# Token sums and Strassen weights at one common byte place in their tiles

## The chip, the cores and the metric

The kernel runs on one core of a Trainium2 chip. A core has a matrix engine (TensorE, PE in the profile, whose weight loads are listed apart as PEld), a vector engine (VectorE, DVE), a scalar engine (ScalarE, ACT), GpSimd (POOL) and a synchronisation engine (SP) from which most transfers are issued. Its on-chip memory has 128 partitions, and every tile is a run of bytes at the same address of each partition; matrix products land in a second memory, PSUM. The metric is the device time of one launch in microseconds (us), lower is better.

## The reference

A two-layer encoder on 512 tokens of width 1024, in 32-bit floats. Each layer has a feed-forward block, a mixer (attention of several kinds in layer 0, banded attention in layer 1), attention to a memory of 256 tokens, and a second feed-forward block. The change touches the four feed-forward blocks:

```python
def rmsnorm(x, g):
    y = x * rsqrt(mean(x * x, axis=-1) + EPS)
    return y * g

def swiglu(x, wg, wu, wd):          # x 512 x 1024, wg and wu 1024 x 2816, wd 2816 x 1024
    return (silu(x @ wg) * (x @ wu)) @ wd

for layer in range(2):
    h = h + 0.5 * swiglu(rmsnorm(h, g1), wg1, wu1, wd1)
    h = h + mixer(rmsnorm(h, gm))
    h = h + memory_attention(rmsnorm(h, gx), rmsnorm(mem, gs))
    h = h + 0.5 * swiglu(rmsnorm(h, g2), wg2, wu2, wd2)
```

## The kernel before

**Products.** Activations are held transposed (features on partitions, tokens along the row). Every 32-bit number that goes into a matrix product is split into a leading part and a rest, and a product of two such numbers is three passes: leading by leading, leading weights by rest of the tokens, and rest of the weights by leading tokens. Tiles whose name ends in `h` hold leading parts, those that end in `l` hold rests: `wh`/`wl` and `sh`/`sl` are weights (two buffers of the first pair, one of the second, used in turn), `xh`/`xl` are tokens. For a weight tile, ScalarE writes the leading part and VectorE the rest, from a raw tile `wf`, `s1` or `s3` that a transfer has filled. In the profile `ps_pa<-xh,wh` is a matmul that streams 256 or 512 columns of `xh` past 128 x 128 weights of `wh` into the PSUM tile `ps_pa`; each matmul has its own weight load.

**A feed-forward block.** The 22 blocks of 128 hidden features are taken in 11 pairs. The first pair (`plain_pair`, L325) is computed directly. The other ten are computed by Strassen's scheme (`open_pair`, `sum_pair`, `cross_pair`, `close_pair`): tokens, input features and gate/up weights are each cut in two, and seven products of half size take the place of eight. Each of the seven is a call of `product` (L452), 24 matmuls of 256 columns: two output blocks, three passes, four blocks of 128 input features. Three of the seven use token parts as they are (`xh`, `xl`, called "11", "21" and "22"), four use sums or differences of token parts (`t1h`, `t1l` to `t4h`, `t4l`). The sums are made once per block in `token_sums`. The weights of a product are the raw quarters (`wf`) or sums of two quarters, which a transfer that adds into the tile, ScalarE and VectorE make (`s1`, `s3`). After some pairs come matmuls of the down projection (`down_products`, L585, 512 columns), in three chunks.

**Order.** The order of TensorE's instructions is the order in which the code issues them; that of the others is set by a scheduler that works from due times. On TensorE a pair is followed by the next in this order: 11, t1, t2, 21, t3, then 11 of the next pair, t4, 22, t1, t2 and so on. So token parts and token sums alternate, but for t1 and t2, which follow each other. In each block ten pairs give 70 products, 280 in the whole program.

**Places.** In what follows the place of an operand is its first byte's address in a partition modulo 512, counted in units of 64 bytes, from 0 to 7. Tiles of 512, 1024 or 2048 numbers take a multiple of 512 bytes, and so do the weight tiles, which are 128 numbers longer than needed (`WIDE`, 1152 numbers, 4608 bytes). So what stands at a tile's start has place 0, and every block of 128 weights or 256 tokens in it has the same place as its first. `operand` (L422) puts a product's weights `place` times 64 bytes (`LINE`, 16 numbers) into their tiles, and `X_PLACE` and `SUM_PLACE` say where:

- products with token parts: tokens at place 0, leading weights at 1, rests at 3;
- products with token sums: tokens at place 1, leading weights at 2, rests at 4. The sums lie in a pool of their own (`f.sp`), whose first tile, `line`, is 64 bytes long and holds nothing;
- all other large matmuls (L325, L585, L638, L687): both operands at place 0.

Of the kernel before, what the change touches and what calls it, by code (L numbers as in the profile page):

```python
# [11 lines left out]
F32 = mybir.dt.float32  # L12
F32R = mybir.dt.float32r
# [6 lines left out]
P = 128  # L20
# [44 lines left out]

LINE = 16
WIDE = 1024 + 8 * LINE
X_PLACE = (1, 3)
SUM_PLACE = (2, 4)

LEAD, REST = ((0, 0), (0, 1)), ((1, 0),)

# [39 lines left out]
class Encoder:  # L112
# [158 lines left out]
    def ffn(self, pre):  # L271


        with ExitStack() as ctx:
            pool = lambda name: ctx.enter_context(self.tc.tile_pool(name=pre + name, bufs=1))
            f = self.f = SimpleNamespace(pre=pre, ctx=ctx, hp=pool("h"), tp=pool("t"), sp=pool("s"), H={}, n=0, last=None)
            R = self.plain_pair()
            ends = [sum(CHUNKS[:c + 1]) // 2 for c in range(len(CHUNKS))]
            c = 0
            pair = self.open_pair(1)  # L280
            R()
            for p in range(1, FB // 2):
                final = p == FB // 2 - 1
                self.sum_pair(pair)
                if p in ends:
                    self.down(c)
                    c += 1
                self.cross_pair(pair)
                if final:
                    early = self.block(c, 0, True)  # L290
                    self.down_products(c, early, LEAD + REST, False)
                    self.close_pair(pair, True)
                    self.down(c, early)
                else:
                    old, pair = pair, self.open_pair(p + 1)
                    self.close_pair(old, False)
                if self.mem_r is None:
                    self.mem_stats(p)
# [71 lines left out]
    def token_sums(self):  # L370


        nc, f = self.nc, self.f
        xs, gain = self.xs, self.col(self.norm)
        half = KB // 2
        one, two = slice(0, 256), slice(256, 512)
        part = lambda t, k: t[:, (k % half) * 256:(k % half) * 256 + 256]
        g = lambda k: gain[:, k:k + 1]

        def combine(out, k, tokens, op, other):  # L380
            nc.vector.scalar_tensor_tensor(part(out, k), self.x[k][:, tokens], g(k), part(other, k), op0=OP.mult, op1=op)

        def parts(name, t, sign=1.0):
            after = None if name == "t1" else f.lowered if name == "t2" else f.gated
            with self.behind(f.factored), self.behind(after):
                h = f.sp.tile([P, 1024], F32R, name=name + "h", tag=name + "h")
                nc.scalar.activation(h, t, AF.Copy, scale=sign)
                l = f.sp.tile([P, 1024], F32R, name=name + "l", tag=name + "l")
                if sign == 1.0:
                    nc.vector.tensor_sub(l, t, h.bitcast(F32))  # L390
                else:
                    nc.vector.scalar_tensor_tensor(l, t, sign, h.bitcast(F32), op0=OP.mult, op1=OP.subtract)
            return [(part(h, k), part(l, k)) for k in range(half)]

        f.sp.tile([P, LINE], F32, name="line", tag="line")
        lead, rest = range(half), range(half, KB)
        room = [f.tp.tile([P, 2048], F32, name="tq", tag="gu", bufs=2) for _ in range(2)]
        t1, t2, x12, t3 = (t[:, o:o + 1024] for t in room for o in (0, 1024))
        for k in lead:
            nc.scalar.activation(part(x12, k), self.x[k][:, two], AF.Copy, scale=g(k))  # L400
        for k in lead:
            combine(t1, k, one, OP.subtract, x12)
        for k in rest:
            combine(t2, k, two, OP.add, t1)
        for k in rest:
            combine(t3, k, two, OP.subtract, x12)
        t4 = x12
        for k in rest:
            combine(t4, k, one, OP.subtract, t2)
        quarters = lambda ks, tokens: [tuple(x[:, tokens] for x in xs[k]) for k in ks]  # L410
        f.B = {"11": quarters(lead, one), "21": quarters(rest, one), "22": quarters(rest, two),
               "1": lambda: parts("t1", t1, -1.0), "2": lambda: parts("t2", t2),
               "3": lambda: parts("t3", t3), "4": lambda: parts("t4", t4)}

    def tokens(self, name):
# [3 lines left out]
            B[name] = B[name]()  # L419
        return B[name]  # L420

    def operand(self, t, place, own=None):  # L422

        nc, f = self.nc, self.f
        if own is None:
            own = f.n % 3 == 2
            f.n += 1
        h, l = [(f.tp if own else self.wp).tile([P, WIDE], F32R, name=n, tag=n, bufs=1 if own else 2)[:, o * LINE:o * LINE + 1024]
                for n, o in zip(("sh", "sl") if own else ("wh", "wl"), place)]
        self.leading = nc.scalar.activation(h, t, AF.Copy)  # L430
        self.parted = nc.vector.tensor_sub(l, t, h.bitcast(F32))  # L431
        return h, l
# [30 lines left out]
    def open_pair(self, p):  # L463
        nc, f = self.nc, self.f
        pair = SimpleNamespace(p=p)
        pair.y = self.bank("pa")
        with self.tc.high_priority():
            pair.w11 = self.raw_quarter(p, 0)
            w = self.operand(pair.w11, X_PLACE)
        self.product(pair.y, w, self.tokens("11"), True)  # L470
        pair.gu = f.tp.tile([P, 2048], F32, name="gu", tag="gu", bufs=2)
        nc.scalar.copy(self.corner(pair, 0, 0), self.halves(pair.y))
        return pair

    def sum_pair(self, pair):

        nc, f, p = self.nc, self.f, pair.p
        pair.z = self.bank("pb")
        with self.tc.high_priority():
            pair.s = f.tp.tile([P, 1024], F32, name="s1", tag="s1", bufs=2)  # L480
            self.fetch(pair.s, p, 3)
            nc.gpsimd.dma_start(pair.s, self.quarter(p, 2), accum_op=OP.add)  # L482
            w = self.operand(pair.s, SUM_PLACE)
        with self.tc.high_priority():
            xs = self.tokens("1")
        self.product(pair.z, w, xs, True)
        with self.tc.high_priority():
            f.lowered = nc.vector.tensor_sub(pair.s, pair.s, pair.w11)
            xs = self.tokens("2")
            w = self.operand(pair.s, SUM_PLACE)  # L490
            f.lowered = self.parted
        self.product(pair.y, w, xs, False)
        nc.scalar.copy(self.corner(pair, 0, 1), self.halves(pair.y))

    def cross_pair(self, pair):
        nc, f, p = self.nc, self.f, pair.p
        with self.tc.high_priority(), self.behind(f.lowered if p == 1 else None):
            pair.w12 = self.raw_quarter(p, 1)
            w = self.operand(pair.w12, X_PLACE)
        x = self.bank("pa")  # L500
        self.product(x, w, self.tokens("21"), True)
        c = self.corner(pair, 0, 0)
        nc.vector.tensor_add(c, c, self.halves(x))
        with self.tc.high_priority():
            s = f.tp.tile([P, 1024], F32, name="s3", tag="s3", bufs=2)
            self.fetch(s, p, 2)
            with self.behind(f.led):
                nc.scalar.activation(s, s, AF.Copy, scale=-1.0)  # L508
            nc.gpsimd.dma_start(s, self.quarter(p, 0), accum_op=OP.add)  # L509
            w = self.operand(s, SUM_PLACE)  # L510
        self.product(pair.y, w, self.tokens("3"), False)
        c = self.corner(pair, 1, 1)
        nc.scalar.copy(c, self.halves(pair.y))
        nc.vector.tensor_add(c, c, self.halves(pair.z))

    def close_pair(self, pair, final):
        nc, f, p = self.nc, self.f, pair.p
        own = False if final else None

        def lower():  # L520
            with self.tc.high_priority():
                w = self.operand(self.raw_quarter(p, 3), SUM_PLACE, own)
            self.product(pair.y, w, self.tokens("4"), False)
            nc.scalar.copy(self.corner(pair, 1, 0), self.halves(pair.y))

        def upper():
            with self.tc.high_priority():
                nc.vector.tensor_sub(pair.s, pair.w12, pair.s)
                w = self.operand(pair.s, X_PLACE, own)
            self.product(pair.z, w, self.tokens("22"), False)  # L530
            c = self.corner(pair, 0, 1)
            nc.vector.tensor_add(c, c, self.halves(pair.z))
# [1027 lines left out]
```

## Time and profile before

| what | value |
|---|---|
| median of three runs | 2098.28 us (2096.92 to 2098.28) |
| the profiled execution | 2099.43 us, span of its instructions 2097.7 us |
| mean granted TensorE clock | 0.996 |
| TensorE busy | 2064.1 us, 98% of the span |
| weight loads busy | 1843.6 us, 88% |
| VectorE busy | 1522.2 us, 73% |
| ScalarE busy | 1141.7 us, 54% |
| transfers | 279.64 MB, 133 GB/s over the span |

A busy matrix engine is not one at its peak: matmuls overlap, so the duration of one (276 ns and more for 256 columns) is longer than the time from its start to the start of the next. The pace is read from the starts, in the timeline. There a row is a run of matmuls of one kind: start in us, time from the first one's start to the last one's end, engine, line, tiles and shapes, and the count.

### The profile page before, as it was taken

What the parts mean: (1) busy time and instruction counts of PE and PEld (TensorE: products, weight loads), DVE (VectorE), ACT (ScalarE), POOL (GpSimd) and SP (SyncE); (2) the same over time, 40 slices, a digit from 0 to 9 for tenths busy, and PEclk for the clock granted to TensorE, in tenths of its full rate; (3) what the DMA queues carried; (4) which work ended last, traced back from release to release, by engine and by line L of the source; (5) the groups of instructions that cost most, each with busy time, mean ns of one, the idle gap of its engine ahead of it and who ended that gap; (6) DMA issues with size and microseconds to landing.
All of it is one profiled execution on the core that took longest, in us unless ns stands there. A gap on an engine that the chain in (4) does not pass through costs nothing.

```text
span 2097.7 us, 32478 instructions
## 1 busy us (share of the span) xinstructions
PE 2064.1 (98%) x12834; PEld 1843.6 (88%) x12834; DVE 1522.2 (73%) x2198; ACT 1141.7 (54%) x1706; POOL 363.2 (17%) x319
## 2 busy tenths in 40 slices
PE   8999999999999999999999999999999999999999
PEld 7989898877788889898989899988888888989997
DVE  8758577589876697685789576675668688857666
ACT  7636345466686575362556354354778566626443
POOL 1101003345431120000020000013453022000000
PEclk9999999999999999999999999999999999999999
DMA  7746535222241266474356466344224225646633
GB/s 236 209 125 179 149 101 181 90 68 69 81 133 62 73 181 181 128 194 131 99 170 175 131 171 181 98 125 149 91 80 131 91 71 151 171 130 180 171 101 93
DMA packets 86120, 279.64 MB, mean 133 GB/s; under 512 B 9680, under 2 KB 12880, under 8 KB 85968
## 3 DMA queue, kind: packets, MB, share of 16 engines
q1 hardware_dynamic: 74448, 235.62, 34.4%
q0 software_dynamic: 11520, 41.95, 11.3%
q8 instruction: 101, 1.65, 0.3%
q14 instruction: 51, 0.42, 0.1%
HBM read 271.24 MB, written 6.29 MB: 132 GB/s over the span
## 4 chain that ended last, share of the span: by engine, by line
PE 89%; DVE 7%; ACT 1%; issue 1%; DMA 1%; POOL 0%; SPq 0%; DVEq 0%; ACTq 0%; POOLq 0%
PE ps_pa L452 26%; PE ps_pa L687 11%; PE ps_pb L452 11%; PE ps_pa L585 11%; PE ps_pb L585 10%; PE ps_pa L638 4%; PE ps_pa L325 3%; PE ps_pb L793 2%; PE ps_pa L1234 2%; PE ps_pb L845 1%; PE ps_pa L1084 1%; PE ps_pb L818 1%; PE ps_pb L638 1%; PE ps_pa L1003 1%; PE ps_pb L325 1%
## 5 line engine op out<-in xcount | busy, mean ns | idle before, releaser
L163 ACT ACTIVATE wh<-wf 128x1024 fp32r<-128x1024 f32 (+2 forms) x211 | 215.2, 1021 | 349.6 <-PE ps_pa L585 97.0
L165 DVE TENSOR_TENSOR wl<-wf,wh 128x1024 fp32r<-128x1024 f32 (+2 forms) x169 | 200.2, 1187 | 49.0 <-ACT wh L163 47.5
L431 DVE TENSOR_TENSOR wl<-s,wh 128x1024 fp32r<-128x1024 f32 x108 | 132.0, 1222 | 67.1 <-ACT wh L430 67.1
L430 ACT ACTIVATE wh<-s 128x1024 fp32r<-128x1024 f32 x108 | 114.4, 1059 | 101.0 <-PE ps_pb L452 35.1
L430 ACT ACTIVATE wh<-wf 128x1024 fp32r<-128x1024 f32 x84 | 88.9, 1059 | 94.7 <-PE ps_pa L452 32.3
L509 POOL DMA_DIRECT2D s<-l_ffn_wq x40 | 35.6, 889 | 528.8 <-ACT s L508 460.8
L165 POOL TENSOR_TENSOR wl<-wf,wh 128x1024 fp32r<-128x1024 f32 x42 | 101.9, 2426 | 141.5 <-ACT wh L163 139.9
L687 PE MATMUL ps_pa<-wh,xh 128*128 128x512 f32 x384 | 123.6, 403 | 0.0
L687 PE MATMUL ps_pa<-wh,xl 128*128 128x512 f32 x384 | 119.9, 393 | 0.0
L687 PE MATMUL ps_pa<-wl,xh 128*128 128x512 f32 x384 | 119.5, 393 | 0.0
L482 POOL DMA_DIRECT2D s<-l_ffn_wq x40 | 35.7, 892 | 437.6 <-PE ps_pa L452 148.1
L431 DVE TENSOR_TENSOR wl<-wf,wh 128x1024 fp32r<-128x1024 f32 x84 | 102.5, 1220 | 6.3 <-ACT wh L430 3.4
L595 DVE TENSOR_TENSOR dn<-ps_pa,R 128x512 f32<-128x512 f32 x48 | 33.1, 689 | 93.2 <-PE ps_pa L585 92.9
L585 PE MATMUL ps_pb<-hh,wh 128*128 128x512 f32 x352 | 95.5, 389 | 0.0
L585 PE MATMUL ps_pb<-hl,wh 128*128 128x512 f32 x352 | 95.4, 389 | 0.0
L585 PE MATMUL ps_pb<-hh,wl 128*128 128x512 f32 x352 | 95.4, 389 | 0.0
L230 POOL TENSOR_TENSOR acc<-acc,sq 128x512 f32<-128x512 f32 (+1 forms) x37 | 51.2, 1383 | 251.5 <-ACT sq L229 250.4
L431 DVE TENSOR_TENSOR sl<-s,sh 128x1024 fp32r<-128x1024 f32 x52 | 64.0, 1232 | 39.5 <-ACT sh L430 39.4
L585 PE MATMUL ps_pa<-hh,wh 128*128 128x512 f32 x328 | 88.8, 390 | 0.0
L585 PE MATMUL ps_pa<-hh,wl 128*128 128x512 f32 x328 | 88.6, 389 | 0.0
L585 PE MATMUL ps_pa<-hl,wh 128*128 128x512 f32 x328 | 88.6, 389 | 0.0
L687 PEld LDWEIGHTS ps_pa<-wh,xl 128*128 128x128 f32 x384 | 72.8, 190 | 16.2
(376 smaller groups left out, 5846.8 us busy)
## 6 DMA issues: line engine op xcount, KB each, us to landing
wf<-l_ffn_wq SPq DMA_DIRECT2D x120, 512.0 KB, 4.0
s<-l_ffn_wq SPq DMA_DIRECT2D x80, 512.0 KB, 4.9
s<-l_ffn_wq POOLq DMA_DIRECT2D x80, 512.0 KB, 7.0
wf<-l_ffn_wd SPq DMA_DIRECT2D x64, 512.0 KB, 4.2
wf<-l_w_in SPq DMA_DIRECT2D x48, 512.0 KB, 3.3
wf<-l_ffn_wd SPq DMA_DIRECT2D x32, 384.0 KB, 3.1
wf<-l_mem_wkv SPq DMA_DIRECT2D x16, 512.0 KB, 3.3
wf<-l_w_out SPq DMA_DIRECT2D x16, 512.0 KB, 3.3
```

The source lines that it names most:

```text
L163: self.leading = nc.scalar.activation(wh[:, sl], w[:, sl], AF.Copy)
L165: eng.tensor_sub(wl[:, sl], w[:, sl], wh.bitcast(F32)[:, sl])
L230: self.summed = (eng or nc.gpsimd).tensor_add(acc[:, :n], acc[:, :n], sq[:, :n])
L325: nc.tensor.matmul(p, w[a][:, k * P:(k + 1) * P], xs[k][c], start=k == order[0] and a == c == 0, stop=k == order[-1] and a == 1)
L430: self.leading = nc.scalar.activation(h, t, AF.Copy)
L431: self.parted = nc.vector.tensor_sub(l, t, h.bitcast(F32))
L452: self.nc.tensor.matmul(bank[:, sl], w[a][:, o:o + P], xs[k][b], start=first and z == a == b == k == 0, stop=z == a == 1 and k == KB // 2 - 1,
L585: self.nc.tensor.matmul(bank, w[a][:, j * P:(j + 1) * P], h, start=j == a == e == 0, stop=j == nb - 1 and (a, e) == ops[-1])
L638: nc.tensor.matmul(banks[dd], a[:, o:o + P], parts(k)[b], start=k == first and a is wh and b == 0, stop=k == last and a is wl)
L687: nc.tensor.matmul(banks[i], xs[k][a][:, i * P:(i + 1) * P], w[b][:, kk * 512:kk * 512 + 512], start=k == a == b == 0, stop=k == KB - 1 an ...
L793: nc.tensor.matmul(bank[:, o:o + n], a, b[:, :n], start=c == 0, stop=c == len(ops) - 1)
L1234: nc.tensor.matmul(p, ws[z][a][:, k * P:(k + 1) * P], xs[k][b], start=k == order[0] and a == b == 0, stop=k == order[-1] and a == 1)
```

## The change

One place for all Strassen products: the token sums now lie in the pool of the block's other tiles (`f.tp`), where each tile starts at a multiple of 512 bytes, and `operand` puts all weights at places 1 and 3. So the products with token sums have tokens at place 0 and weights at 1 and 3, as those with token parts had and have. Within a product the distance from tokens to weights is what it was, 64 and 192 bytes.

```diff
-X_PLACE = (1, 3)
-SUM_PLACE = (2, 4)
+PLACE = (1, 3)
...
-            f = self.f = SimpleNamespace(pre=pre, ctx=ctx, hp=pool("h"), tp=pool("t"), sp=pool("s"), H={}, n=0, last=None)
+            f = self.f = SimpleNamespace(pre=pre, ctx=ctx, hp=pool("h"), tp=pool("t"), H={}, n=0, last=None)
...
         def parts(name, t, sign=1.0):
...
-                h = f.sp.tile([P, 1024], F32R, name=name + "h", tag=name + "h")
+                h = f.tp.tile([P, 1024], F32R, name=name + "h", tag=name + "h")
                 nc.scalar.activation(h, t, AF.Copy, scale=sign)
-                l = f.sp.tile([P, 1024], F32R, name=name + "l", tag=name + "l")
+                l = f.tp.tile([P, 1024], F32R, name=name + "l", tag=name + "l")
...
-        f.sp.tile([P, LINE], F32, name="line", tag="line")
...
-    def operand(self, t, place, own=None):
+    def operand(self, t, own=None):
...
-                for n, o in zip(("sh", "sl") if own else ("wh", "wl"), place)]
+                for n, o in zip(("sh", "sl") if own else ("wh", "wl"), PLACE)]
...
-            w = self.operand(pair.s, SUM_PLACE)
+            w = self.operand(pair.s)
...
-            w = self.operand(pair.w12, X_PLACE)
+            w = self.operand(pair.w12)
```

In the same way every other call of `operand` loses its `place`. With the pool gone, some tiles of a block get other addresses: `t1h` moves from byte 192576 to 175104, `sh` from 175104 to 191488, `s3` from 184320 to 200704, `t3h` from 208960 to 208896. `wh`, `wl`, `wf`, `s1`, `xh` and `xl` stay.

No instruction is added, removed or put elsewhere in its queue, on any engine. What each waits for is the same too, but at one place: in the first feed-forward block of layer 1, TensorE waits once for the transfers that filled the tiles of the block before (the names that begin with `DMA`). Before, it did so ahead of t2's first product:

```order
L343 MATMUL ps_pb<-ident,factor 128x128 x3
L452 MATMUL ps_pb<-t1h,wh 128x256 [waits Activation_49]
L452 MATMUL ps_pb<-t1h,wh 128x256 x3
L452 MATMUL ps_pb<-t1l,wh 128x256 [waits DVE_49]
...
L452 MATMUL ps_pb<-t1h,wl 128x256 x4
L452 MATMUL ps_pa<-t2h,sh 128x256 [waits DMAHW0_49,DMASW7_49,DMAHW1_49,DMASW6_49,DMAHW2_49,DMASW5_49,DMAHW3_49,DMASW4_49,DMAHW4_49,DMASW3_49,DMAHW5_49,DMASW2_49,DMAHW6_49,DMASW1_49,DMAHW7_49,DMASW0_49,Activation_49]
L452 MATMUL ps_pa<-t2h,sh 128x256 x3
```

Now it does so ahead of t1's (lines are two lower in the changed file):

```order
L342 MATMUL ps_pb<-ident,factor 128x128 x3
L450 MATMUL ps_pb<-t1h,wh 128x256 [waits DMAHW0_49,DMASW7_49,DMAHW1_49,DMASW6_49,DMAHW2_49,DMASW5_49,DMAHW3_49,DMASW4_49,DMAHW4_49,DMASW3_49,DMAHW5_49,DMASW2_49,DMAHW6_49,DMASW1_49,DMAHW7_49,DMASW0_49,Activation_49]
L450 MATMUL ps_pb<-t1h,wh 128x256 x3
L450 MATMUL ps_pb<-t1l,wh 128x256 [waits DVE_49]
...
L450 MATMUL ps_pb<-t1h,wl 128x256 x4
L450 MATMUL ps_pa<-t2h,sh 128x256 [waits Activation_49]
L450 MATMUL ps_pa<-t2h,sh 128x256 x3
```

The same 16 waits, for the same transfers, stand 24 matmuls earlier.

More of the change, by code (lines that the diff above doesn't have):

```diff
@@ L468, in open_pair @@
             pair.w11 = self.raw_quarter(p, 0)
-            w = self.operand(pair.w11, X_PLACE)
+            w = self.operand(pair.w11)
         self.product(pair.y, w, self.tokens("11"), True)
@@ L489, in sum_pair @@
             xs = self.tokens("2")
-            w = self.operand(pair.s, SUM_PLACE)
+            w = self.operand(pair.s)
             f.lowered = self.parted
@@ L509, in cross_pair @@
             nc.gpsimd.dma_start(s, self.quarter(p, 0), accum_op=OP.add)
-            w = self.operand(s, SUM_PLACE)
+            w = self.operand(s)
         self.product(pair.y, w, self.tokens("3"), False)
@@ L521, in lower @@
             with self.tc.high_priority():
-                w = self.operand(self.raw_quarter(p, 3), SUM_PLACE, own)
+                w = self.operand(self.raw_quarter(p, 3), own)
             self.product(pair.y, w, self.tokens("4"), False)
@@ L528, in upper @@
                 nc.vector.tensor_sub(pair.s, pair.w12, pair.s)
-                w = self.operand(pair.s, X_PLACE, own)
+                w = self.operand(pair.s, own)
             self.product(pair.z, w, self.tokens("22"), False)
```

## The prediction

> **What bounds the kernel now.** I began with the page's busy shares and the chain of work that ended last.
>
> ```profile
> PE 2064.1 (98%) x12834; PEld 1843.6 (88%) x12834; DVE 1522.2 (73%) x2198; ACT 1141.7 (54%) x1706; POOL 363.2 (17%) x319
> ...
> PE 89%; DVE 7%; ACT 1%; issue 1%; DMA 1%; POOL 0%; SPq 0%; DVEq 0%; ACTq 0%; POOLq 0%
> ```
>
> The matrix engine is the bound: 98% of the span, 89% of the chain. The change touches only operands of L452, so I asked next how busy the engines are in a stretch that is nothing but Strassen pairs, and then who waits for whom at L452. The row of the windows view has the stretch, its length, the busy us (and instructions) of PE, PEld, DVE, ACT and POOL, the granted clock, the share and rate of the transfers; the others come from the view of line 452.
>
> ```profile
> 875.00:950.00 75.00, 75.00 (x650) 75.00 (x650) 60.08 (x58) 46.32 (x53) 6.92 (x8) 1.00 0.71 191
> ...
>   DVE wl L431: 4.3, 5
>   ACT gu L513: 4.2, 3
>   DVE gu L514: 1.1, 4
>   DVE sl L431: 0.3, 1
>   ACT gu L493: 0.2, 1
> ...
>   ACT wh L430: 101.0, 76
> ```
>
> In 75 us PE is never idle and its clock is full, while VectorE works 60.08 us (80%) and ScalarE 46.32. In the whole program PE stood still at L452 only 14 times, 10.1 us together. The other way round ScalarE waited 101.0 us, 76 times, for PE to give a `wh` buffer back: the operands are ahead. So time is won here only if the matmuls follow each other faster, and the timeline of PE tells whether they can. One pair, the first row of each product, with some rows between:
>
> ```profile
> 906.01 0.63 PE L452 MATMUL ps_pb<-t1h,wh 128*128 128x256 f32 x4
> 906.48 0.63 PE L452 MATMUL ps_pb<-t1l,wh 128*128 128x256 f32 x4
> ...
> 907.89 0.62 PE L452 MATMUL ps_pb<-t1l,wh 128*128 128x256 f32 x4
> 908.34 0.62 PE L452 MATMUL ps_pb<-t1h,wl 128*128 128x256 f32 x4
> 908.80 0.62 PE L452 MATMUL ps_pa<-t2h,wh 128*128 128x256 f32 x4
> 909.25 0.62 PE L452 MATMUL ps_pa<-t2l,wh 128*128 128x256 f32 x4
> ...
> 911.52 0.64 PE L452 MATMUL ps_pa<-xh,sh 128*128 128x256 f32 x4
> ...
> 914.31 0.63 PE L452 MATMUL ps_pa<-t3h,wh 128*128 128x256 f32 x4
> ...
> 917.10 0.64 PE L452 MATMUL ps_pa<-xh,wh 128*128 128x256 f32 x4
> ...
> 919.89 0.63 PE L452 MATMUL ps_pa<-t4h,sh 128*128 128x256 f32 x4
> ...
> 922.68 0.64 PE L452 MATMUL ps_pb<-xh,wh 128*128 128x256 f32 x4
> ...
> 925.47 0.63 PE L452 MATMUL ps_pb<-t1h,wh 128*128 128x256 f32 x4
> ```
>
> Start to start, t2's product takes 908.80 to 911.52, 2.72 us; each of the other six takes 2.79, with no idle time. The loss is at a product's head: four matmuls take 0.47 us there (906.01 to 906.48), and 0.45 near its end (907.89 to 908.34) and all through t2 (908.80 to 909.25). t2 is the only product whose predecessor, t1, has its operands at the same places; the others come after a switch between places 0/1/3 and 1/2/4. So I read 0.07 us as the price of a switch.
>
> Is it the place, or any change of tiles? Outside the products the same engine shows both. From the last matmuls of an output projection (L638) to the first of a feed-forward block (L325), tiles and line change and all places stay 0. From the down projection (L585) to a product with `xh`, tokens stay at place 0 and only weights move, to 1 and 3:
>
> ```profile
> 735.82 0.39 PE L638 MATMUL ps_pb<-ol,wh 128*128 128x512 f32 x1
> 736.05 0.39 PE L638 MATMUL ps_pb<-oh,wl 128*128 128x512 f32 x1
> 736.27 1.07 PE L325 MATMUL ps_pa<-xh,wh 128*128 128x512 f32 x4
> 737.18 1.07 PE L325 MATMUL ps_pa<-xl,wh 128*128 128x512 f32 x4
> ...
> 142.92 0.63 PE L452 MATMUL ps_pa<-xh,wh 128*128 128x256 f32 x4
> ...
> 145.71 0.51 PE L452 MATMUL ps_pa<-t3h,wh 128*128 128x256 f32 x3
> ```
>
> The first pays nothing: 736.27 to 737.18 is 0.91 us for four, 0.227 each, as before it (735.82 to 736.05, 0.23). The second pays in full: 2.79. Places go with the loss, new tiles alone do not.
>
> **The change part by part.** *Switches.* Ten pairs of seven products give 69 borders in a block; 10 are t1 to t2; at 4 something else stands between (down projections after two pairs and in the last one, four transposes after the very first product). That leaves 55 a block, 220, less one with transposes of the memory statistics: 219 switches between products, all of which the change turns into the border that t1 and t2 have now. At 0.07 us that is 15.3 us. Where PE stood still, the wait can have hidden the switch; without the 14 waits it is 205 times 0.07, 14.4. I take the middle, 14.8.
>
> *Borders that stay.* Twelve products after a down projection and four after L325 still start after another place, and keep their 0.07. The 16 borders from a product into a down projection become weights 3 to 0 with tokens still, which this trace nowhere has. What they cost now:
>
> ```profile
> 99.38 1.55 PE L585 MATMUL ps_pa<-hh,wh 128*128 128x512 f32 x6
> 100.76 1.52 PE L585 MATMUL ps_pa<-hl,wh 128*128 128x512 f32 x6
> 102.12 1.07 PE L585 MATMUL ps_pb<-hh,wh 128*128 128x512 f32 x4
> ```
>
> 1.38 us for the first six and 1.36 for the next: 0.02. The ends are 0 and the 0.07 of the row above, so minus 0.3 to plus 0.8 us for 16; nearest is the same line's own row, no difference, 0.
>
> *Writes at other places.* ScalarE and VectorE now write sums' weights and tokens 64 bytes lower. The page has both kinds (`wf` mostly goes to 1 and 3, `s` mostly to 2 and 4):
>
> ```profile
> L431 DVE TENSOR_TENSOR wl<-s,wh 128x1024 fp32r<-128x1024 f32 x108 | 132.0, 1222 | 67.1 <-ACT wh L430 67.1
> L430 ACT ACTIVATE wh<-s 128x1024 fp32r<-128x1024 f32 x108 | 114.4, 1059 | 101.0 <-PE ps_pb L452 35.1
> L430 ACT ACTIVATE wh<-wf 128x1024 fp32r<-128x1024 f32 x84 | 88.9, 1059 | 94.7 <-PE ps_pa L452 32.3
> ...
> L431 DVE TENSOR_TENSOR wl<-wf,wh 128x1024 fp32r<-128x1024 f32 x84 | 102.5, 1220 | 6.3 <-ACT wh L430 3.4
> ```
>
> 1059 ns against 1059 and 1222 against 1220: nothing, either way. `sh`, `s3` and the sums swap regions, all still at multiples of 512 bytes; no queue and no wait changes with it, so 0.
>
> *The one wait that moves* stands ahead of t1 in layer 1's first block and asks for transfers into tiles that the block before has already used up. Queued behind it is all of PE. At its old spot it cost nothing, since t2 there keeps its pace:
>
> ```profile
> 1105.76 0.62 PE L452 MATMUL ps_pa<-t2h,sh 128*128 128x256 f32 x4
> ...
> 1108.47 0.64 PE L452 MATMUL ps_pa<-xh,wh 128*128 128x256 f32 x4
> ```
>
> 2.71 us. I take 0.
>
> *What is late next.* A pair shrinks from 19.46 us (906.01 to 925.47) to 7 times 2.72, 19.04, or 2.2%. VectorE's 80% becomes 82%, the transfers' 0.71 becomes 0.73: the cover holds in the long stretches. In the first pairs of a block, where the lead is still being built, the 0.42 us may be lost in waits: at most two pairs in four blocks, 3.4 us, at least 0. The row of 14 idle times says that few places are that tight; I take 0.6.
>
> **Sum.** 14.8 less 0.6 is 14.2. From the profiled execution's 2099.43 that gives 2085.2. The median of the runs lies 1.15 below that execution, so 2084.1.
>
> **The rivals.** *Places don't matter* (2098.3, within 0.2%). The slow head could come with the switch between token parts and token sums, two sets of tiles far apart in memory, which the change keeps: six of seven products stay at 2.79. For it: places and sets of tiles switch at the same borders in this trace. Against it: 736.27, where tiles change for nothing, and 142.92, where `xh` follows other tiles and pays the same 0.07 that it pays after sums. The Trainium skill's page "SBUF — State Buffer", section "SBUF: two separate sides", says that PE and ACT have ports of their own and never wait on anyone, with contention only at the port pair of VectorE and GpSimd; by that no place in a tile could matter. The same skill's "TensorE: Matmul & The Clock Gate", section "Back-to-back issue gap", gives a warm gap by the column count alone, 109 ns at 256 columns as worked out from its formula. The trace disagrees with both: 0.47/4 and 0.45/4, 118 and 113 ns, at one column count and a clock of 1.00.
>
> *Given back to late transfers* (2091.5). One place shows the mechanism: a quarter lands late, ScalarE stands in front of it at L508, and behind it waits the copy L513 that frees PE's bank.
>
> ```profile
> 1810.47 1.06 ACT L508 ACTIVATE s<-s 128x1024 f32<-128x1024 f32 x1 [3.35 <-DMA s<-l_ffn_wq]
> ...
> 1812.38 0.57 ACT L513 COPY gu<-ps_pa 128x512 f32<-128x512 f32 x1
> ...
> 1813.00 1.05 PE L452 MATMUL ps_pa<-t4h,wh 128*128 128x256 f32 x4 [1.89 <-ACT gu L513]
> ...
> 1817.47 0.63 PE L452 MATMUL ps_pb<-xh,sh 128*128 128x256 f32 x4
> ```
>
> PE idles 1.89 us and then needs 4.47 us for a product of 2.72: 3.6 us. A faster PE asks earlier; two such events more make 2084.1 plus 7.3. Against it: one in 40 pairs now.
>
> *The switch is what restores the pace* (2109, slower). The two read streams may drift into collision in a long run at places 0/1/3, and a new place may be what lines them up again. The longest fast run at 256 columns is the end of t1 and all of t2, some 32 matmuls; now there would be runs of hundreds. If the head's pace became the pace of all, a product would take 6 times 0.47, 2.82: 0.03 more for 219, 0.10 more for the 40 of t2, 10.6 us. It decides from the point where a run outlasts 32 matmuls. Against it: the down projection's long runs at constant places hold 1.36 for six.
>
> **How the numbers follow.** Forecast 0.79; given back 0.08; no effect 0.08; slower 0.05. About 0.2%, 4.2 us, is what can be told from no change: faster 0.87, same 0.08, slower 0.05. The likeliest case's own range is 2081.5 to 2087.5 (15.3 plus the 0.3 of the borders and a pace read to 10 ns, down to 14.4 less 3.4). Up to 2092 it takes in what is given back, and leaves 0.13 and the odd miss outside.
>
> **What would show it.** In the view of line 452 the median of `xh,wh`, `t1h,wh`, `t3h,wh` and `t4h,wh` falls to that of `t2h,wh`. In the timeline every product inside a run starts 2.72 us after the one before, and a pair takes 19.04; products after L585 and L325 still take 2.79. Durations of L430 and L431 stay. If all products keep 2.79, place was not the cause; if they reach 2.72 and the time falls by less than 11 us, look for new idle time at L452 in the first pairs of a block; if t2 itself slows, the two streams drift.

## The result and the profile after

The changed kernel takes 2086.13 us (median; 2085.85 to 2088.27), the kernel before 2097.84 us beside it (2096.92 to 2098.28). The ratio is 0.9947, with a 95% interval of 0.993 to 0.9964: 11.7 us less. The profiled execution took 2088.27 us (span 2086.4, mean granted clock 0.997), 11.2 us less than the one before.

The page of the changed kernel, busy shares and chain of work that ended last:

```profile
PE 2049.9 (98%) x12830; PEld 1829.5 (88%) x12834; DVE 1519.1 (73%) x2198; ACT 1141.4 (55%) x1706; POOL 362.8 (17%) x319
...
PE 87%; DVE 8%; ACT 2%; issue 2%; DMA 1%; POOL 0%; SPq 0%; DVEq 0%; ACTq 0%; POOLq 0%
```

PE is busy 14.2 us less; VectorE and ScalarE work as long as they did. The view of the product's line in the changed kernel gives the duration of one matmul in ns as least, median and largest:

```profile
L450 PE MATMUL ps_pa<-xh,wh x448: 276/276/285, 32.4 to 2039.6; 128*128 128x256 f32 x150
```

The same view of the kernel before has 281 as the median, and so it is for the products with `t1h`, `t3h` and `t4h`:

```profile
L452 PE MATMUL ps_pa<-xh,wh x448: 276/281/285, 31.5 to 2050.8; 128*128 128x256 f32 x150
```

The timeline of PE shows what that does to a pair. The first rows of t1, t2, 21, t3 and, three products later, 22 in the changed kernel (and t1's second row):

```profile
903.70 0.62 PE L450 MATMUL ps_pb<-t1h,wh 128*128 128x256 f32 x4
904.15 0.62 PE L450 MATMUL ps_pb<-t1l,wh 128*128 128x256 f32 x4
...
906.42 0.62 PE L450 MATMUL ps_pa<-t2h,wh 128*128 128x256 f32 x4
...
909.14 0.62 PE L450 MATMUL ps_pa<-xh,sh 128*128 128x256 f32 x4
...
911.86 0.62 PE L450 MATMUL ps_pa<-t3h,wh 128*128 128x256 f32 x4
...
920.02 0.62 PE L450 MATMUL ps_pb<-xh,wh 128*128 128x256 f32 x4
```

From t1 to t3 each product takes 2.72 us, the next three together 8.16 (3 times 2.72). The first four matmuls of t1 take 0.45 (903.70 to 904.15) where they took 0.47. But PE now waits more at that line. The view of the line for the matmuls alone (without the weight loads) groups their waits by what ended them (us, times). In the changed kernel:

```profile
  ACT gu L511: 3.0, 4
  DVE wl L429: 2.3, 3
  ACT gu L491: 0.7, 1
  ACT sh L428: 0.3, 1
```

and in the kernel before:

```profile
  ACT gu L513: 1.9, 1
  DVE wl L431: 1.8, 2
```

That is 6.3 us in 9 waits, where it was 3.7 in 3. The largest part of the growth, 1.1 of 2.6 us, stands at `gu L511`, the copy that frees PE's bank after the t3 product. One of its chains, early in the program, in the timeline of the changed kernel (in brackets the idle time ahead, and what ended it):

```profile
66.91 1.06 ACT L506 ACTIVATE s<-s 128x1024 f32<-128x1024 f32 x1 [1.95 <-DMA s<-l_ffn_wq]
...
67.88 1.04 ACT L428 ACTIVATE sh<-s 128x1024 fp32r<-128x1024 f32 x1
...
68.83 0.56 ACT L511 COPY gu<-ps_pa 128x512 f32<-128x512 f32 x1
...
69.44 0.74 PE L450 MATMUL ps_pa<-t4h,wh 128*128 128x256 f32 x4 [0.64 <-ACT gu L511]
```

ScalarE stands 1.95 us in front of a quarter that has not landed, for the negation at L506. Behind it in its queue the t3 copy waits, and PE waits for the copy. In the kernel before, t4 had no idle time ahead of it, and the copy was 1.27 us early (66.54 plus 0.57 to 68.38):

```profile
66.54 0.57 ACT L513 COPY gu<-ps_pa 128x512 f32<-128x512 f32 x1
...
68.38 0.63 PE L452 MATMUL ps_pa<-t4h,wh 128*128 128x256 f32 x4
```

The quarter's transfer tells the difference. It is the one that SP issues for `s` in the window from 55 us to the product, at 60.15 before and at 60.69 now. The transfer view of that window, with KB and us from issue to landing, in the kernel before:

```profile
s<-l_ffn_wq SPq DMA_DIRECT2D x1, 512.0 KB, 4.4
```

and in the changed one:

```profile
s<-l_ffn_wq SPq DMA_DIRECT2D x1, 512.0 KB, 6.1
```

It is issued 0.54 us later and takes 1.7 us longer; an adding transfer of GpSimd was issued at 59.99 before and 59.98 now, so it had 0.7 us of a lead over SP's where it had 0.16. That their order or overlap is what took the 1.7 us is argued, not shown; nor is it shown that a faster PE caused it here, so early that the changed kernel is still behind the one before (its first matmul of the products starts at 32.4 us, where it was 31.5).

### The profile page after: what moved, and what is told of

Read it like the earlier page. It is cut to its first block, busy times and chain, and to the rows that moved or that the text cites. A ratio compares the mean times of both kernels' runs of the same rounds, so it can differ in the third digit from the quotient of the medians.

```text
span 2086.4 us, 32474 instructions
## 1 busy us (share of the span) xinstructions
PE 2049.9 (98%) x12830; PEld 1829.5 (88%) x12834; DVE 1519.1 (73%) x2198; ACT 1141.4 (55%) x1706; POOL 362.8 (17%) x319
## 4 chain that ended last, share of the span: by engine, by line
PE 87%; DVE 8%; ACT 2%; issue 2%; DMA 1%; POOL 0%; SPq 0%; DVEq 0%; ACTq 0%; POOLq 0%
PE ps_pa L450 23%; PE ps_pa L685 11%; PE ps_pa L583 11%; PE ps_pb L583 10%; PE ps_pb L450 10%; PE ps_pa L636 4%; PE ps_pa L324 3%; PE ps_pb L791 2%; PE ps_pa L1232 2%; PE ps_pb L843 1%; PE ps_pa L1082 1%; PE ps_pb L816 1%; PE ps_pb L636 1%; PE ps_pa L1001 1%; PE ps_pb L324 1%
```

## The experiments

All runs below keep the order of instructions on every engine, but for the three that leave the negation out or give it to another engine. In those a rest of weights and a reduction on VectorE, some 28 us from the start, change places too; in the one with GpSimd, so do a few neighbours on VectorE and in SP's queue. "Product" means the 24 matmuls of one call; its length is the median of the products without a wait, from its first start to the next one's, worked out from the starts in the timeline.

### Which half of the switch costs?

Before the change, tokens and weights both move by 64 bytes at a switch. One experiment leaves the tokens' switch out, so that only weights switch (1 and 3 to 2 and 4, tokens always at 0):

```diff
-                h = f.sp.tile([P, 1024], F32R, name=name + "h", tag=name + "h")
+                h = f.tp.tile([P, 1024], F32R, name=name + "h", tag=name + "h")
...
-                l = f.sp.tile([P, 1024], F32R, name=name + "l", tag=name + "l")
+                l = f.tp.tile([P, 1024], F32R, name=name + "l", tag=name + "l")
...
-        f.sp.tile([P, LINE], F32, name="line", tag="line")
```

> All tokens stay at place 0; only the weights of the products with token sums go to 2 and 4, those with token parts to 1 and 3. Theory: a border costs 0.07 us when a place changes, and the row after the down projection says that a change of the weights alone is enough. Then six of seven products take 2.79 us again and the time is that of before, about 2097.8. Rival, only the tokens' place counts: 2.72 everywhere, 2086.1. If each of the two streams pays its own share, something like 2.755 and 2092.

Measured: 2105.1 us against 2098.82; ratio 1.0028 (1.0018 to 1.0038). Slower than before. The other leaves the weights at 1 and 3 in all products and lets only tokens switch, 0 to 1:

```diff
-SUM_PLACE = (2, 4)
+SUM_PLACE = (1, 3)
```

> The token sums go back to place 1, all weights stay at 1 and 3. Theory (any change of place costs): 2.79 us for six of seven products, about 2097.8. Rival, only the weights' place counts: 2.72, 2086.1. Here the distance from tokens to weights also changes, from 64 to 0 bytes for the leading part: if that alone slows the steady pace, t2 too leaves 2.72.

Measured: 2102.22 us; ratio 1.0016 (1.0007 to 1.0025). Slower too. The timeline of PE with only weights switching:

```profile
910.36 0.63 PE L451 MATMUL ps_pb<-t1h,wh 128*128 128x256 f32 x4
...
913.21 0.64 PE L451 MATMUL ps_pa<-t2h,wh 128*128 128x256 f32 x4
...
916.06 0.63 PE L451 MATMUL ps_pa<-xh,sh 128*128 128x256 f32 x4
...
918.85 0.63 PE L451 MATMUL ps_pa<-t3h,wh 128*128 128x256 f32 x4
```

and with only tokens switching:

```profile
909.36 0.63 PE L452 MATMUL ps_pb<-t1h,wh 128*128 128x256 f32 x4
...
912.20 0.64 PE L452 MATMUL ps_pa<-t2h,wh 128*128 128x256 f32 x4
...
915.05 0.64 PE L452 MATMUL ps_pa<-xh,sh 128*128 128x256 f32 x4
...
917.79 0.63 PE L452 MATMUL ps_pa<-t3h,wh 128*128 128x256 f32 x4
```

t2, which follows t1 at the same places, takes 2.85 us in both (913.21 to 916.06; 912.20 to 915.05), where it took 2.72 before and after. So there is a second effect. For the first run neither my theory nor its rivals had it; what was expected of the second names it as a possibility. Each half alone also changes the distance from tokens to weights of the products with sums, from 64 and 192 bytes to 128 and 256 in the first run, to 0 and 128 in the second. The fast pace is lost there without a switch. What one half of a switch costs can't be read from these two. A `xh` product after sums takes 2.74 in the second run (915.05 to 917.79), and in the first 2.79 after t2 (916.06 to 918.85), but 2.73 after t3 and t4: these heads are cheaper than the 0.07 I counted for any change of place, and I have no reading for that.

### Is a constant place enough?

Two variants of the changed kernel keep one place throughout, but another distance: 128 and 256 bytes, and 0.

```diff
-PLACE = (1, 3)
+PLACE = (2, 4)
```

> All tokens at place 0, all weights of Strassen products at 2 and 4. Theory, only constancy counts: 2.72 us for all products inside a run, 2086.1. Rival, the distance of 64 and 192 bytes from tokens to weights is what makes 2.72 possible: the pace of the head, 2.82 us a product, 280 times 0.10 more, about 2114.

```diff
-PLACE = (1, 3)
+PLACE = (0, 0)
```

> All operands at place 0, so no place changes anywhere in a feed-forward block. Theory, only constancy counts: 2.72 us for all products, those after the down projection and after the first pair too, and 1.36 for the first six matmuls of the down projection: 16 times 0.07 and 16 times 0.02 less, about 2084.7. Rival, the two streams need an offset at 256 columns: up to 2.82 us a product, about 2114.

Measured: 2113.08 us at 2 and 4, ratio 1.0066 to the kernel before (1.0051 to 1.0081), and 2123.45 us at 0 and 0, ratio 1.0116 (1.0101 to 1.0131). The timeline of PE at 2 and 4:

```profile
912.88 0.63 PE L450 MATMUL ps_pb<-t1h,wh 128*128 128x256 f32 x4
...
915.72 0.63 PE L450 MATMUL ps_pa<-t2h,wh 128*128 128x256 f32 x4
...
918.56 0.63 PE L450 MATMUL ps_pa<-xh,sh 128*128 128x256 f32 x4
```

and at 0 and 0:

```profile
912.66 0.64 PE L450 MATMUL ps_pb<-xh,sh 128*128 128x256 f32 x4
...
915.54 0.64 PE L450 MATMUL ps_pb<-t1h,wh 128*128 128x256 f32 x4
```

Products take 2.84 and 2.88 us, one like the other: 118 and 120 ns a matmul, where the changed kernel has 113 (2.72/24). Between Strassen products nothing switches, and the pace never gets better in a run of pairs. So constancy is not enough. The distance decides whether there is a fast pace at all; where there is, a switch of both operands by 64 bytes costs its 0.07 us on top. Only one good distance was tried at 256 columns, 64 and 192 bytes.

The Trainium skill's page "SBUF — State Buffer", section "SBUF: two separate sides", says of contention in this memory that PE never waits on anyone. It says nothing of a cost of operand addresses. In these two runs and the changed kernel the same products differ by up to 0.16 us by the operands' addresses alone.

### Does a switch by 256 bytes cost as much?

If places count modulo 512 bytes, as I had numbered them, a switch by 256 bytes is a switch like any other; if they repeat every 256 bytes, it is none. Three variants of the kernel before, each with the good distance in all products (modulo 256 bytes). In the first, the sums' tokens lie at 4 and their weights at 5 and 7:

```diff
-SUM_PLACE = (2, 4)
+SUM_PLACE = (5, 7)
...
-        f.sp.tile([P, LINE], F32, name="line", tag="line")
+        f.sp.tile([P, 4 * LINE], F32, name="line", tag="line")
```

> The kernel before with the sums' tokens at place 4 and their weights at 5 and 7, in place of 1 and 2 and 4: distances within a product as before, the switch between products 256 bytes and not 64. If any change of place starts the same settling: 2.79 us a product, 2098. If the settling makes up the bytes of the switch (64 bytes up cost 64 ns, 64 bytes down 72 ns): a product some other time than 2.79, up to four times 0.07 more, 2.72 plus 0.28, and 2144.

In the second, all tokens are at 0, and only weights go between 1 and 3 and 5 and 7 (the edit of the first experiment above, and this):

```diff
-SUM_PLACE = (2, 4)
+SUM_PLACE = (5, 7)
```

> All tokens at place 0; weights of products with token parts at 1 and 3, with token sums at 5 and 7, which is 256 bytes higher. Theory: places count modulo 256 bytes, so nothing switches and the distance is as good: 2.72 us for all products inside a run, about 2086. Rival, only a move of both by 256 bytes together is free, or a distance of 320 and 448 bytes is a bad one like 128 and 256: 2.79 to 2.85 us for the products with sums, 2098 to 2105.

In the third, both switch by 128 bytes:

```diff
-SUM_PLACE = (2, 4)
+SUM_PLACE = (3, 5)
...
-        f.sp.tile([P, LINE], F32, name="line", tag="line")
+        f.sp.tile([P, 2 * LINE], F32, name="line", tag="line")
```

> The kernel before with the sums' tokens at place 2 and their weights at 3 and 5: the distance within a product is kept, a switch is 128 bytes. If a switch by anything but 256 bytes starts a settling of 0.07 us: 2.79 us a product and 2098. If a settling lasts as the distance to the nearest multiple of 256 bytes: up to twice as long, 2.86 us, 219 times 0.07 more and 2113. If it depends on direction, products with sums and with parts differ.

Measured: 2086.88 us, ratio 0.9945 (0.993 to 0.9961), for both by 256 bytes; 2087.22, ratio 0.9945 (0.9924 to 0.9965), for the weights alone by 256; 2097.73, ratio 0.9997 (0.9987 to 1.0008), for both by 128. The timeline of PE with both switching by 256 bytes:

```profile
907.33 0.62 PE L452 MATMUL ps_pa<-xh,sh 128*128 128x256 f32 x4
...
910.05 0.62 PE L452 MATMUL ps_pa<-t3h,wh 128*128 128x256 f32 x4
...
912.77 0.62 PE L452 MATMUL ps_pa<-xh,wh 128*128 128x256 f32 x4
```

and by 128 bytes:

```profile
906.25 0.64 PE L452 MATMUL ps_pb<-t1h,wh 128*128 128x256 f32 x4
...
909.04 0.62 PE L452 MATMUL ps_pa<-t2h,wh 128*128 128x256 f32 x4
...
911.76 0.64 PE L452 MATMUL ps_pa<-xh,sh 128*128 128x256 f32 x4
...
914.55 0.64 PE L452 MATMUL ps_pa<-t3h,wh 128*128 128x256 f32 x4
```

A switch by 256 bytes is free, for both operands together and for the weights alone: 2.72 throughout, and the whole gain of the change comes without giving up the switch. Neither time that was expected of the first variant had this. A switch by 128 costs the 0.07 of one by 64 (2.79, and 2.72 for t2 alone). So for these products places repeat every 256 bytes, and "Places don't matter" falls as well: the first variant keeps `f.sp` and both sets of tiles, and only adds 192 bytes to the place.

### The borders that stay, and the large matmuls

Twelve products follow a down projection, whose operands are at 0 and 0, and keep their 0.07. Here the weights of the first pair and of the down projection go to 1 and 3 as well:

```diff
-    def wtile(self):
-        return [self.wp.tile([P, c], dt, name=n, tag=n, bufs=b)
-                for n, dt, c, b in (("wf", F32, 1024, 3), ("wh", F32R, WIDE, 2), ("wl", F32R, WIDE, 2))]
+    def wtile(self, place=(0, 0)):
+        w, h, l = [self.wp.tile([P, c], dt, name=n, tag=n, bufs=b)
+                   for n, dt, c, b in (("wf", F32, 1024, 3), ("wh", F32R, WIDE, 2), ("wl", F32R, WIDE, 2))]
+        return [w] + [t[:, o * LINE:o * LINE + 1024] for t, o in zip((h, l), place)]
...
-            return self.wload(src, n), self.bank2()
+            return self.wload(src, n, None, PLACE), self.bank2()
```

> The changed kernel, with the weights of the first pair and of the down projection also at 1 and 3, so that nothing in a feed-forward block changes place but the few transposes. Theory, as the runs before have left it (fast pace at a distance of 64 and 192 bytes, 16 matmuls to settle after a change of place): the 12 products after the down projection fall from 2.79 to 2.72 us, the first six matmuls of the down projection from 1.38 to 1.36: 1.2 us less than the changed kernel, 2085. Rival, 512 columns want weights and tokens at one place: the down projection and the first pair lose their 0.227 us a matmul, up to 0.236 as in their slow rows, 2424 matmuls times 0.009 or 22 us more.

Measured: 2098.34 us, ratio 1.0001 to the kernel before (0.9992 to 1.0011): 12.2 us more than the changed kernel, on another occasion. A product after a down projection takes 2.73 instead of 2.79, so these borders did hold a cost of place, less than 1 us for 16. The loss is in the 512-column matmuls. Rows of six of them in the down projection of this run:

```profile
100.42 1.56 PE L584 MATMUL ps_pa<-hl,wh 128*128 128x512 f32 x6
101.82 1.56 PE L584 MATMUL ps_pb<-hh,wh 128*128 128x512 f32 x6
```

and of the changed kernel:

```profile
102.28 1.52 PE L583 MATMUL ps_pa<-hl,wh 128*128 128x512 f32 x6
103.64 1.52 PE L583 MATMUL ps_pb<-hh,wh 128*128 128x512 f32 x6
```

From start to start six take 1.40 us instead of 1.36. Over the whole line the mean is 232.9 ns a matmul instead of 226.9 (worked out from all its starts without a wait between them), and 6.0 ns for the line's 2111 matmuls is 12.7 us, about as much as was lost. At 512 columns 0 and 0 is the better distance, and 64 and 192 bytes, the best of those tried at 256 columns, is worse.

### What was given back

To see the gain without the waits behind L506, the negation is left out of both kernels, so that ScalarE stands in front of no transfer there (t3's weights are then a sum of two quarters, not a difference):

```diff
-            with self.behind(f.led):
-                nc.scalar.activation(s, s, AF.Copy, scale=-1.0)
```

> The kernel before without ScalarE's negation of the fetched quarter s3 (L508), so a sum is made where a difference belongs and the output is another; ScalarE no longer waits there for a transfer, and its copy that frees TensorE's bank does not stand behind that wait. Theory (some of the gain was given back there): TensorE's waits at L452 for the copy go, the time falls by 2 to 6 us, to 2092 to 2096.

> The changed kernel without the same negation; the output is another in the same way. Theory: what the change wins over the previous run, with no such wait in either, is the whole of the settling, 14 to 15 us, where it was 11.7 with the negation: 2078 to 2081. Rival, the missing 3 us went elsewhere (VectorE, the transfers themselves): the two differ by 11.7 again.

Measured: 2094.62 us from the kernel before, ratio 0.9986 (0.9976 to 0.9995), and 2081.36 us from the changed one, ratio 0.9923 (0.9907 to 0.994). The change is worth 13.3 us between these two, where 14 to 15 were expected and 11.7 if the negation had no part in it. Waits of PE's matmuls at the product's line, first without the negation in the kernel before:

```profile
  DVE wl L431: 1.8, 2
  ACT gu L493: 0.6, 1
```

then in the changed one:

```profile
  DVE wl L429: 2.2, 3
  ACT gu L491: 0.6, 1
```

No wait for the t3 copy is left, and the two lists differ by 0.4 us instead of 2.6. The time from the first to the last Strassen matmul of each of the four blocks, worked out from the timelines of the profiled executions, in us, tells what the waits do (the last three rows are the variants of the section on 256 bytes, all with the negation):

| kernel | block 1 | block 2 | block 3 | block 4 | sum |
|---|---|---|---|---|---|
| before | 286.2 | 286.4 | 285.3 | 289.5 | 1147.4 |
| after | 285.4 | 282.9 | 281.7 | 286.1 | 1136.1 |
| before, no negation | 286.0 | 286.3 | 285.2 | 285.8 | 1143.3 |
| after, no negation | 282.4 | 282.3 | 281.5 | 282.2 | 1128.4 |
| both by 256 bytes | 284.1 | 282.4 | 283.8 | 284.4 | 1134.8 |
| weights alone by 256 | 283.1 | 284.3 | 281.8 | 283.9 | 1133.1 |
| both by 128 bytes | 286.7 | 286.1 | 285.2 | 287.3 | 1145.2 |

Without the negation each block gains 3.6 to 4.0 us, 14.9 in all. With it, blocks 2 and 3 gain 3.5 and 3.6 and block 4 gains 3.4, but block 1 only 0.8. The negation costs the kernel before 4.1 us in these blocks and the changed one 7.7. So between these executions 3.6 us of the gain went back, most of it in block 1: there PE has five waits, 2.0 us together, in the changed kernel, and none over 0.05 us in the kernel before. Three of the five are for the t3 copy, and after each wait PE's first matmuls are slow (0.74 us for the four at 69.44, where 0.62 is usual). Between medians the negation costs less: 3.6 us before (2098.18 to 2094.62 beside each other) and about 4.8 after (2086.13 to 2081.36, on different occasions). A difference as small as this one is not clear of the noise, since the ratio of each changed kernel is known to about 3.5 us either way. The profiled execution of the changed kernel is also the longest of its runs, by 2.1 us over the median.

The other rows bear the direction out, but not the size or the place. With products of 2.72 us the negation costs 7.7, 6.4 and 4.7 us (over 1128.4); with products of 2.79, 4.1 and 1.9 (over 1143.3). PE's waits for the t3 copy are 3.0, 3.8 and 1.8 us in those three fast kernels and 1.9 and 0.6 in the two slower ones; 1.4 and 2.1 where only weights or only tokens switch; 0.3 with all at 2 and 4, and none with all at 0 and 0, the slowest. So on the whole a faster PE loses more behind the negation, but by how much is open: between 0.6 and 5.8 us as the rows are paired, one execution each. The waits move about too: the one at 69.44 us stands in neither of the other two fast kernels.

Nor has a wait one price. In the prediction's rows 1.89 us at 1813.00 were followed by a product of 4.47 us. The windows view gives a granted clock of 0.56 from 1813 to 1815 us and of 0.67 from there to 1817.5, and 1.00 on both sides. The changed kernel pays the same at that pair: 1.96 us, then 4.46 at clocks of 0.58 and 0.69. With both switching by 256 bytes the wait there is 1.99 us, but the clock stays at 1.00 and the product takes 2.83.

A version that keeps the arithmetic gives the negation to GpSimd, so that ScalarE's copies no longer stand behind the transfer:

```diff
-                nc.scalar.activation(s, s, AF.Copy, scale=-1.0)
+                nc.gpsimd.tensor_scalar(s, s, -1.0, None, op0=OP.mult)
```

> The changed kernel with the negation of s3 on GpSimd, which issues the next transfer into s3 itself, in place of ScalarE; nothing is left out. ScalarE's copies that free TensorE's bank no longer stand behind a wait for a transfer. Theory: as without the negation, TensorE's waits for those copies go and the time falls from 2086 to 2081 to 2083. Rival, GpSimd takes over 2.4 us for what took ScalarE 1.06 (its rate for a subtraction of this size) and s3 comes that much later, so that TensorE waits for the weights of t3's product: 2086 or more.

Measured: 2084.92 us (2084.57 to 2086.39), ratio 0.9935 to the kernel before (0.9919 to 0.9952). The expected 2081 to 2083 was missed. By its median it is the fastest version that computes the whole reference, but only 1.2 us below the changed kernel, and the two intervals overlap. The group of the negation in this run:

```profile
L506 POOL TENSOR_SCALAR s<-s 128x1024 f32<-128x1024 f32 x40 | 136.2, 3405 | 507.2 <-DMA s<-l_ffn_wq 470.1 <-DVE hl L367 22.0 <-DVE gs L356 14.9
```

The wait for the transfer now stands on GpSimd (470.1 us, most of which costs nothing), but one negation takes 3.4 us instead of 1.06. The waits of PE's matmuls at L450 fall to 1.3 us and none is for the t3 copy; 1.1 of them are for L470, the copy after a pair's first product. The four blocks sum to 1131.7 us, 4.4 less than in the changed kernel and 3.3 more than without the negation.

## Why the prediction was right, and where it was off

**2084.1 was forecast, 2086.13 measured**: in the range, and in the likeliest case's own (2081.5 to 2087.5). The gain was put at 14.2 us and is 11.7.

**The switches: right.** 219 at 0.07 us were to go; all products inside a run fell to 2.72, a pair to 19.04 (7 times 2.72), the medians from 281 to 276. The 14.8 us are met by the 14.9 of the blocks without the negation; between the medians of those two kernels it is 13.3. But the lower end of that term was misread: the view of L452 lists weight loads and matmuls alike, and of its 14 waits (10.1 us) 11 are of weight loads, three of these beside a matmul's wait at the same moment. PE's matmuls waited 3 times, 3.7 us, and only one of the three stands at a head. So the count gives 218 to 219 switches, about 15.3 us, and the closeness of 14.8 to 14.9 is in part luck.

**The borders that stay: right.** The first six matmuls of a down projection take 1.39 us in the changed kernel (1.38 before), and a product after it 2.78:

```profile
100.89 1.55 PE L583 MATMUL ps_pa<-hh,wh 128*128 128x512 f32 x6
102.28 0.39 PE L583 MATMUL ps_pa<-hl,wh 128*128 128x512 f32 x1
...
144.44 0.63 PE L450 MATMUL ps_pa<-xh,wh 128*128 128x256 f32 x4
...
147.22 0.62 PE L450 MATMUL ps_pa<-t3h,wh 128*128 128x256 f32 x4
```

**Writes at other places, the moved wait: right.** The two groups that write sums' weights in the changed kernel stand as they were:

```profile
L428 ACT ACTIVATE wh<-s 128x1024 fp32r<-128x1024 f32 x108 | 114.7, 1062 | 98.2 <-PE ps_pb L450 33.6
...
L429 DVE TENSOR_TENSOR wl<-s,wh 128x1024 fp32r<-128x1024 f32 x108 | 132.0, 1222 | 65.6 <-ACT wh L428 65.2
```

No idle time ended by a transfer stands in the list at L450, and t1 there follows the transposes as closely as before, so the 16 waits that went ahead of t1 cost nothing.

**What is late next: mis-sized.** The term "I take 0.6" for the first pairs of a block measured 3.6 us in the profiled executions, and 1.6 between medians (13.3 of gain without the negation, 11.7 with it), which alone is within the noise. The mechanism was named, in the rival "Given back to late transfers", with its place, the negation ahead of the t3 copy; what I left out was that it could be paid in part in the likeliest case. My bound of 3.4 lies near 3.6 by chance: it took two pairs in each of four blocks, and 2.8 of the 3.6 us went in the first block alone, where PE's waits stand between the 14th and the 33rd of 70 products. The ground for 0.6 was that idle times at L452 were few; they were fewer than I read, but that list counts waits of PE, and says nothing of how near ScalarE stood to making PE wait. At the product of 68.38, PE did not wait, and the copy it needed was only 1.27 us early, behind a transfer whose landing moved by more than that. I had not read how early such copies were. The rival's price of 3.6 us an event was that of a wait with a lowered clock behind it, which a wait as long need not have (its sum, 2084.1 plus 7.3, is 2091.4).

**"The switch is what restores the pace": fell.** Runs of hundreds of matmuls at 0, 1 and 3 hold 2.72.

**The reason behind the 0.07: right for this change, too simple beyond it.** "Places go with the loss, new tiles alone do not" holds. But I numbered places modulo 512 bytes and took any change for a switch; a change by 256 is none. And I took t2's pace for that of constant places, where it is that of constant places at a good distance: with constant places at a bad one, the kernel is slower than with all its switches (2113 and 2123 against 2098).

**Open.** Why a `xh` product after t3 and t4 paid almost nothing where only weights switched; and what in PE's reading of its two operands makes distance and switch cost. No run tells the parts of the memory apart, so I give no mechanism. Open too is what sets how much goes back behind the negation in one execution.

## What to carry to other kernels

Where TensorE is the bound, read its pace from start to start at one column count, over several products: a few ns a matmul that come and go at borders can point to operand addresses, and can then be removed without touching any instruction. Choose the distance from moving to stationary operand by trial for each column count, then keep both constant modulo the period (256 bytes here). And before a bound engine is made faster, look for the engine ahead of it that stands in front of a transfer with a bank's release queued behind it: that is where part of the gain can go back.

## What the runs showed of the hardware

- With a weight load for each matmul, 256 columns take 113 ns at a distance of 64 and 192 bytes (leading and rest weights) between tokens and weights, 118 at 128 and 256, and 120 at 0, all at a mean granted clock of 0.997 to 0.998. The Trainium skill's page "TensorE: Matmul & The Clock Gate", section "Back-to-back issue gap", has no address in its formulas. An estimate from its formula for an isolated matmul on a warm clock, 109 ns at 256 columns, is below all three.
- A switch of both operands by 64 or 128 bytes costs 0.07 us; one by 256 bytes costs nothing (2.79 and 2.72 us a product). In the kernel before, the cost is spread over the first 16 of 24 matmuls (four take 0.47 us, then 0.45).
- At 512 columns the order is reversed: 227 ns from start to start at 0 and 0, 233 at 64 and 192 bytes.
- After waits of 1.89 and 1.96 us PE's granted clock fell to 0.56 and 0.58 in two executions; after 1.99 us at the same product it stayed at 1.00 in a third.
- A negation of 128 x 1024 numbers took 3.4 us on GpSimd and 1.06 us on ScalarE.
